# Feed-forward entry: own space for the first weights, banks and copy targets, three blocks begun ahead, and GpSimd on part of the last activations

## The chip, the core and the metric

The kernel runs on one core of a Trainium2 chip. A core has a matrix engine (TensorE, PE in the profile), a vector engine (VectorE, DVE), a scalar engine (ScalarE, ACT), GpSimd (POOL) and a queue engine (SyncE, SP) that here issues all transfers. On-chip memory is SBUF; matmuls write into the eight banks of PSUM. Every engine works through its own list of instructions in order and stops at a wait until a semaphore is reached. The metric is the device time of the run in microseconds; lower is better.

## The reference, cut to what matters

One transformer block on 1024 tokens of width 1024. A mixing half (dilated attention and a gated delta rule) gives `y`; the change lies behind it, where the residual is formed, normalised, and sent through the feed-forward layer:

```python
y = jnp.concatenate([y_attn, y_delta], axis=-1) @ w_out[l]
x = x + g1 * y
h = _rmsnorm(x, norm_ffn_g[l]) * (1.0 + sc2) + sh2
y = (jax.nn.silu(h @ w_gate[l]) * (h @ w_up[l])) @ w_down[l]
x = x + g2 * y
return _rmsnorm(x, final_norm_g)
```

`w_gate` and `w_up` are 1024 x 2816, `w_down` is 2816 x 1024, all in 32-bit floats.

## The kernel before, in words

**Precision.** Each matmul operand is split in two: a rounded high part (`...h`, made by a ScalarE cast) and the rest (`...l`, a subtraction of the high part from the source). A product is three matmuls: high x high, high x low, low x high. A slab of weights is 128 x 512; it takes a transfer, a cast (`wh`, line 1502) and a subtraction (`wl`, line 1503, on VectorE).

**Residual stage.** A first loop (line 1339) has already added half of the output projection. The loop at line 1415 runs over two halves of the tokens (`hf`, 512 tokens each) and eight tiles of the width (`d`). For each it splits a slab of `w_out` (`wsplit`: ring `wr` of three raw slabs, rings `wh` and `wl` of five, subtraction on GpSimd, line 216), runs 12 matmuls (line 567), adds the result to the residual tile `x2[d, hf]` on VectorE (line 1429), transposes the tile on TensorE for the later residual (`x2_turn`, lines 1382 to 1389, up to two tiles behind), and sums the squares: ScalarE squares, GpSimd or VectorE adds (lines 1437 to 1441).

**Norm.** After each half, eight tiny matmuls (`ssq`, line 1451) sum the squares over the partitions, ScalarE takes the root, VectorE the reciprocal, VectorE spreads it on a diagonal (`dg`, line 1454), TensorE broadcasts it (`rsb`, line 1458) and ScalarE copies it out (`rs`, line 1459). `normed2` (line 1469) scales each tile with `rs` on VectorE (line 1471) and adds the shift on ScalarE (line 1474). The first half's norm lies inside the second half's matmuls. The second half's lies at the end of the stage, ahead of all feed-forward matmuls.

**Feed-forward as seven products.** The layer's products are done by a scheme of seven products in place of eight, over a 2 x 2 division of weights (quarters `a11`, `a12`, `a21`, `a22`) and activations. The activation side needs seven operands of four tiles each, all split high and low: `H11` and `H21` (first token half alone, ready early) and `H22`, `T1`, `T2`, `T3`, `T4` (sums and differences that need the second token half). `h2_split` (line 1404) makes them: a ScalarE cast (line 1406) and a VectorE subtraction (line 1407). In the last of them, `T4`, VectorE does the cast as well. The differences are VectorE instructions of `sub` (line 1519).

**Order of the feed-forward work.** There are 11 blocks `f`, each with a gate side (`wg`) and an up side (`wu`). `up_first` (line 1526) does a side's two products with `H11` and `H21` (24 matmuls, banks `a` and `b`); `rest_begin` does `T2` and `T1` (24 matmuls, bank `c`), and `up_rest` does `T3`, `H22`, `T4` (36 matmuls), with copies `u2` and `r5` taken out of the banks between (lines 1566 and 1568). `AHEADF` blocks have their first parts done ahead (`early`, line 1639), since these need no second half; `begun` then starts block 0's rest; the loop over all blocks follows. A block begun ahead loads its raw slabs a second time for its rest. All these matmuls have the line 1513.

**What sets the order.** The program is written in order and a scheduler lays out each engine's list by priority (`urgent()` raises it); within a list the order is fixed when it runs. A tile that takes over memory of an earlier one waits until that one's last reader is done. Three such places matter here. The feed-forward weights' pool `wq` and the operands' pool `pt` lie where the residual stage's operands and weight slabs lay. The feed-forward banks `pq` lie where the banks of the stage before lay. And the pool `po2`, with `u2` and `r5`, is opened after `sx.close()`, so it lies where the residual tiles `x2` lay.

Of the kernel before, what the change touches and what calls it, by code (L numbers as in the profile page):

```python
# [18 lines left out]
P = 128  # L19
# [10 lines left out]
EARLY = 1  # L30
LEVELS = ("qd", 4), ("z1", 36)
TAIL = 4
AHEADF = 2
XB, ETB, AT, AV = 5, 4, 1, 3
EPS = 1e-6
BIG = 1e30
# [33 lines left out]
def build(tc, I, out):  # L70
# [21 lines left out]
    def urgent():  # L92
        return tc.high_priority(offset=6000)
# [1284 lines left out]
    pf, sf = pool("pf")  # L1378
    po, so = pool("po")
    ps_, ss_ = pool("ps_")  # L1380
    px, sx = pool("px")
    def x2_turn(d, hf, t):

        ps = tbank(f"x2t{d}_{hf}")
        for b in range(4):
            nc.tensor.transpose(ps[:, b * P : (b + 1) * P], t[:, b * P : (b + 1) * P], ident)
        xt = px.tile([P, 4, P], F32, name=f"xt2_{d}_{hf}", tag="m", bufs=5)
        nc.scalar.copy(xt.rearrange("p b d -> p (b d)"), ps)
# [10 lines left out]
    def h2_block(p, name):  # L1399
        HB[name] = [  # L1400
            tuple(p.tile([P, HALF], F32R, name=f"{name}{w}{k}", tag=f"{name}{w}{k}") for w in "hl") for k in range(4)
        ]

    def h2_split(name, k, src, lo_eng, copy=None):
        hi, lo = HB[name][k]
        (copy or nc.scalar.copy)(hi, src)
        lo_eng.tensor_tensor(out=lo, in0=src, in1=hi.bitcast(F32), op=ALU.subtract)
# [6 lines left out]
    for i, (ks, hf) in enumerate(((range(4), 0), (range(4), 1), (range(4, 8), 1), (range(4, 8), 0))):  # L1414
        for d in ks:
            x2[d, hf] = px.tile([P, HALF], F32, name=f"x2_{d}_{hf}", tag=f"x{i}", bufs=4)

    for hf in range(2):
        cs = slice(hf * HALF, (hf + 1) * HALF)
        if hf == 1:  # L1420
            acc = px.tile([P, HALF], F32, name="acc2_1", tag="m", bufs=5)
        for d in range(KT):
            slabs = [(wsplit(I["wo"][d, 0], 512, f"wo{d}_0_{hf}"), 0)]
            t = x2[d, hf]
            nc.sync.dma_start(t, _.xp[2 * d + hf])
            ps = (gbank, sbank)[d % 2](f"wo{d}_0_{hf}")
            run(gemm(ps, slabs, yh, yl, cs))
            with urgent():
                nc.vector.scalar_tensor_tensor(
                    out=t, in0=ps, scalar=mod[:, 16 + d : 17 + d], in1=t, op0=ALU.mult, op1=ALU.add,  # L1430
                )
            behind.append((d, hf, t))
            if len(behind) > 2:
                with tc.issue_after(last[0].ins):
                    x2_turn(*behind.pop(0))
            if d == 0:
                nc.scalar.activation(acc, t, AF.Square)
            else:
                sq = px.tile([P, HALF], F32, name=f"sq2_{hf}_{d}", tag="m", bufs=5)
                nc.scalar.activation(sq, t, AF.Square)  # L1440
                (nc.vector if d > 5 else nc.gpsimd).tensor_tensor(out=acc, in0=acc, in1=sq, op=ALU.add)
        while behind:
            x2_turn(*behind.pop(0))

        ps, pb = ybank(f"ssq2_{hf}"), abank(f"rsb2_{hf}")
        r4 = r8[:, 4 * hf : 4 * hf + 4]
        rs = po.tile([P, HALF], F32, name=f"rs2_{hf}", tag="p1", bufs=4)
        dg = po.tile([P, 4, P], F32, name=f"dg2_{hf}", tag="p1", bufs=4)
        with urgent():
            for tb in range(4):  # L1450
                nc.tensor.matmul(ps[:, tb : tb + 1], acc[:, tb * P : (tb + 1) * P], ones[:, 0:1], start=True, stop=True)
            nc.scalar.activation(r4, ps[:, 0:4], AF.Sqrt, bias=eps1, scale=1.0 / D)
            nc.vector.reciprocal(r4, r4)
            nc.vector.tensor_tensor(
                out=dg, in0=ident.unsqueeze(1).to_broadcast([P, 4, P]),
                in1=r4.unsqueeze(2).to_broadcast([P, 4, P]), op=ALU.mult,
            )
            nc.tensor.matmul(pb, ones, dg.rearrange("p b t -> p (b t)"), start=True, stop=True)
            nc.scalar.copy(rs, pb)
        if hf == 1:  # L1460
            sy.close()
            spv.close()
            swp.close()
            wq, swq = pool("wq", side="right")
            pt, st_ = pool("pt", side="right")
            for name in ("H22", "T1", "T2", "T3", "T4"):
                h2_block(pt, name)

        def normed2(d):
            t = x2[d, hf]  # L1470
            nc.vector.scalar_tensor_tensor(
                out=t, in0=t, scalar=G2[:, d : d + 1], in1=rs, op0=ALU.mult, op1=ALU.mult
            )
            nc.scalar.activation(t, t, AF.Identity, bias=mod[:, 24 + d : 25 + d])

        if hf == 0:
            for d in range(KT):
                normed2(d)
                h2_split(("H11", "H21")[d // 4], d % 4, x2[d, 0], nc.vector)


    spg.close()
    pq, spq = pool("pq", space=PSUM)

    def fbank(name):
        return pq.tile([P, HALF], F32, name=name, tag="f", bufs=8)

    def raw_load(src, name, more=False):
        if more:
# [16 lines left out]
    def up_mm(ps, src, name, what, first=True):  # L1506

        wh, wl = parts(src, name)
        for k in range(4):
            w0 = slice(k * P, (k + 1) * P)  # L1510
            bh, bl = HB[what][k]
            for n_, (a, b) in enumerate(((wh, bh), (wh, bl), (wl, bh))):
                nc.tensor.matmul(  # L1513
                    ps, a[:, w0], b, start=(first and k == 0 and n_ == 0), stop=(k == 3 and n_ == 2),
                    skip_group_check=True,
                )
# [6 lines left out]

    def up_first(f, w, raws):

        a, b = fbank(f"{w}a{f}"), fbank(f"{w}b{f}")
        up_mm(a, raws[0], f"{w}{f}_11", "H11")
        p1 = po.tile([P, HALF], F32, name=f"p1_{w}{f}", tag="p1", bufs=4)  # L1530
        with urgent():
            nc.scalar.copy(p1, a)
        up_mm(b, raws[1], f"{w}{f}_12", "H21")
        with urgent():
            add(p1, b, p1)
        return a, p1
# [18 lines left out]
    def up_rest(f, w, a, raws):  # L1555

        a11, a12 = raws
        if (f, w) == (0, "wg"):
            (s1, s2, a21, a22), c = rest0, begun
        else:  # L1560
            a21, a22 = (raw_load(I[w][NF + f, s], f"{w}{f}_2{s}", True) for s in range(2))
            s1, s2 = rest_sums(po2 if w == "wu" else ps_, f, w, raws, a21, a22)
            c = rest_begin(f, w, a, (s1, s2))
        u2, r5 = (po2.tile([P, HALF], F32, name=f"{w}{f}_u{i}", tag="u", bufs=4) for i in (2, 5))
        with urgent():
            nc.scalar.copy(u2, a)
# [15 lines left out]
    def gate_first(f, w):  # L1582
        raws = raws_first(f, w)
        a, c11 = up_first(f, w, raws)
        return a, c11, raws
# [58 lines left out]

    t2 = []
    for k in range(4):
        normed2(k)
        normed2(4 + k)
# [10 lines left out]
        sub(x2[k, 1], x2[4 + k, 1], x2[k, 1])  # L1659
        h2_split("T3", k, x2[k, 1], nc.vector)  # L1660
    for k in range(4):
        h2_split("H22", k, x2[4 + k, 1], nc.vector)
    for k in range(4):
        sub(x2[4 + k, 0], x2[4 + k, 0], t2[k])
        h2_split("T4", k, x2[4 + k, 0], nc.vector, nc.vector.tensor_copy)
    sx.close()
    po2, so2 = pool("po2")
    for f in range(NF):
        up_end(f, early[f] if f < AHEADF else None)
        for i in {0: (), 1: (), NF - 2: (NF - 4, NF - 3), NF - 1: (NF - 2, NF - 1)}.get(f, (f - 2,)):  # L1670
            wd_sums(i)
    so2.close()
    ss_.close()
    so.close()
    sf.close()
# [206 lines left out]
```

## Time and profile before

| what | value |
|---|---|
| median of three runs | 1454.71 us (1454.52 to 1459.43) |
| the profiled execution's own time | 1459.26 us |
| its span | 1457.5 us |
| TensorE busy | 1381.9 us (95%) |
| VectorE, ScalarE, GpSimd busy | 872.7, 668.8, 284.5 us |
| mean granted TensorE clock | 0.975 |
| feed-forward entry in the span | from about 798 to 856 us |

The span is counted from the first to the last instruction. A busy share is an average over stages of very different kinds. So the stretch around the entry is read by itself: TensorE's instructions in order of time show where it stops, the view of waits names what it stopped for, and the lists of VectorE, ScalarE and GpSimd in the same stretch show what they were doing. In the profile a timeline row is start, length, engine, line, operation, tiles written and read, and the idle time before it with what ended it. TensorE's rows overlap, since a matmul's result comes some time after the next has begun; the pace is the distance between starts. The rows of a table by stretch give the length, then for PE, PEld, DVE, ACT and POOL the busy time and (x) the instructions, then the granted TensorE clock, the DMA share and GB/s.

### The profile page before, as it was taken

To read this page: it belongs to the slowest core of one execution; us is meant where nothing else is said; L and a number is where in the kernel's file an instruction comes from. 1 tells how busy PE (TensorE), PEld (TensorE's weight loads), DVE (VectorE), ACT (ScalarE), POOL (GpSimd) and SP (SyncE) were. 2 spreads that over 40 slices of the span, in tenths; PEclk is the share of its full clock that TensorE was granted. 3 is DMA by queue.
4 is the path that set the end of the run, shared out by engine and by line. 5 is a ranking of instruction groups with operands and counts; after the bars stand their busy time and mean duration, and the time that the engine had idled before them with its cause. 6 is when DMAs were issued, how large, how long until landed. Compare 5 with 4: busy or idle time off the path is not lost.

```text
span 1457.5 us, 24558 instructions
## 1 busy us (share of the span) xinstructions
PE 1381.9 (95%) x8984; PEld 1121.6 (77%) x8984; DVE 872.7 (60%) x1676; ACT 668.8 (46%) x1279; POOL 284.5 (20%) x267
## 2 busy tenths in 40 slices
PE   7998989998999989999999889999999999999997
PEld 4777857787888768778877668888888888888886
DVE  3686762665746151466426985767666676565477
ACT  3487513348233363566337733333333333444446
POOL 1343412243323333344244000000000000000000
PEclk9998999998999989999999989999999999999999
DMA  8736464465531626643275443545454465866566
GB/s 306 251 106 175 134 192 142 146 197 168 157 107 56 179 78 181 169 121 95 92 226 168 136 151 117 192 137 175 148 167 156 155 207 182 277 211 202 198 218 238
DMA packets 171345, 244.64 MB, mean 168 GB/s; under 512 B 33014, under 2 KB 76327, under 8 KB 171224
## 3 DMA queue, kind: packets, MB, share of 16 engines
q1 hardware_dynamic: 171224, 243.07, 53.0%
q8 instruction: 71, 1.16, 0.3%
q14 instruction: 50, 0.41, 0.1%
HBM read 180.25 MB, written 67.48 MB: 170 GB/s over the span
## 4 chain that ended last, share of the span: by engine, by line
PE 63%; DVE 6%; DMA 4%; ACT 3%; issue 2%; POOL 1%; SPq 0%; ACTq 0%; DVEq 0%; POOLq 0%
PE wga L1513 8%; PE wua L1513 8%; PE X L1699 6%; PE g_a L567 5%; PE wuc L1513 4%; PE wgc L1513 4%; PE Z L1699 4%; PE wo L567 4%; PE g_va L590 3%; PE y L1293 3%; PE tr L1276 2%; PE Y L1699 2%; PE wub L1513 2%; PE wgb L1513 2%; PE S L1252 1%
## 5 line engine op out<-in xcount | busy, mean ns | idle before, releaser
L1503 DVE TENSOR_TENSOR wl_db<-wr_db,wh_db 128x512 fp32r<-128x512 f32 x77 | 53.2, 691 | 75.6 <-ACT wh_db L1502 75.5
L1502 ACT CAST wh_db<-wr_db 128x512 fp32r<-128x512 f32 x77 | 47.9, 622 | 97.8 <-PE X L1699 41.3
L1699 PE MATMUL X<-wl_db,wh_da 128*128 128x512 f32 x176 | 68.5, 389 | 0.0
L1699 PE MATMUL X<-wh_db,wl_da 128*128 128x512 f32 x176 | 68.5, 389 | 0.0
L1699 PE MATMUL X<-wh_db,wh_da 128*128 128x512 f32 x176 | 68.5, 389 | 0.0
L1263 POOL TENSOR_SCALAR X<-X,sc 128x128 f32<-128x128 f32 (+7 forms) x64 | 47.6, 747 | 70.6 <-DVE sc L1262 56.2
L1261 ACT ACTIVATE X<-X,sc 128x128 f32<-128x128 f32 (+7 forms) x64 | 49.6, 776 | 22.4 <-DVE sc L1256 17.2
L1256 DVE CUSTOM_DVE_ANT_0 X<-S,ng 128x512 f32<-128x512 f32 (+3 forms) x64 | 36.8, 586 | 35.0 <-PE S L1253 26.3
L567 PE MATMUL wo<-yh,wh_wo 128*128 128x512 f32 x128 | 52.2, 409 | 3.7 <-ACT yh L1359 2.1
L1503 DVE TENSOR_TENSOR wl_da<-wr_da,wh_da 128x512 fp32r<-128x512 f32 x77 | 52.7, 686 | 1.2 <-ACT wh_da L1502 1.2
L567 PE MATMUL g_a<-hh,wh_a 128*128 128x512 f32 x128 | 51.4, 401 | 0.0
L567 PE MATMUL g_a<-hl,wh_a 128*128 128x512 f32 x128 | 51.1, 399 | 0.0
L567 PE MATMUL g_a<-hh,wl_a 128*128 128x512 f32 x128 | 51.0, 398 | 0.0
L567 PE MATMUL wo<-yl,wh_wo 128*128 128x512 f32 x128 | 51.0, 398 | 0.0
L567 PE MATMUL wo<-yh,wl_wo 128*128 128x512 f32 x128 | 50.5, 396 | 0.0
L1502 ACT CAST wh_da<-wr_da 128x512 fp32r<-128x512 f32 x77 | 47.4, 616 | 5.9 <-PE wua L1513 5.8
L1222 DVE SCALAR_TENSOR_TENSOR QS<-raw,QS 64x1024 fp32r<-64x1024 f32 x8 | 12.6, 1571 | 61.4 <-ACT QS L1221 61.4
L1502 ACT CAST wh_wg_s<-wg_s 128x512 fp32r<-128x512 f32 x33 | 20.5, 622 | 58.1 <-PE wuc L1513 22.6
L1293 PE MATMUL y<-et,va 128*64 128x128 f32 x576 | 46.7, 289 | 0.0
L1276 PE MATMUL tr<-ident,X 128*128 128x128 f32 x288 | 45.0, 282 | 1.6 <-ACT et L1281 1.2
L1502 ACT CAST wh_wg<-wr_wg 128x512 fp32r<-128x512 f32 x33 | 20.4, 622 | 51.4 <-issue 20.0
L1293 PEld LDWEIGHTS y<-et,va 128*64 128x64 f32 x576 | 35.0, 142 | 10.4 <-issue 8.8
(530 smaller groups left out, 4391.4 us busy)
## 6 DMA issues: line engine op xcount, KB each, us to landing
wr_da<-ao_d SPq DMA_DIRECT2D x77, 256.0 KB, 3.1
wm<-in_wada SPq DMA_DIRECT2D x64, 256.0 KB, 3.6
wr_wg<-in_wg SPq DMA_DIRECT2D x48, 256.0 KB, 2.9
wr_wu<-in_wu SPq DMA_DIRECT2D x48, 256.0 KB, 2.7
ao_d<-a SPq DMA_DIRECT2D x44, 256.0 KB, 2.2
wr_wd<-in_wdn SPq DMA_DIRECT2D x44, 256.0 KB, 3.0
wr_db<-wt_d SPq DMA_DIRECT2D x44, 256.0 KB, 2.6
ao_d<-as SPq DMA_DIRECT2D x33, 256.0 KB, 2.0
```

Of the source, the lines that this page charges most:

```text
L567: last[0] = nc.tensor.matmul(ps, a[:, w0], b[k0 + k4][:, cs], start=(i == 0), stop=(i == n - 1))
L590: last[0] = nc.tensor.matmul(ps[:, :n], a[k][:, ts_], b[:, w0], start=(i == 0), stop=(i == 23))
L1252: nc.tensor.matmul(ps[:, 0 : c1 - c0], QS[:, qs], KS[:, c0:c1], start=True, stop=False)
L1256: nc.vector.tensor_tensor_reduce(out=X[:, c0:c1], in0=ps[:, 0 : c1 - c0], in1=ng[:, u + c0 : u + c1], scale=1.0, scalar=(3e38 if m is None ...
L1261: nc.scalar.activation(X[:, 0:nk], X[:, 0:nk], AF.Exp, scale=-1.0, bias=m, accum_out=sc[:, 2:3])
L1263: nc.gpsimd.tensor_scalar(out=X[:, 0:nk], in0=X[:, 0:nk], scalar1=sc[:, 3:4], scalar2=0.0, op0=ALU.mult, op1=ALU.add)
L1276: nc.tensor.transpose(ps[:, (kb - c0) * P : (kb - c0 + 1) * P], X[:, kb * P : kb * P + P], ident)
L1293: nc.tensor.matmul(yps[64 * e : 64 * e + 64, yc], va[:, kb, 64 * e : 64 * e + 64], ets[e][:, kb, :], start=(kb == 0), stop=(kb == qb),)
L1502: nc.scalar.copy(hi, src)
L1503: (eng or nc.vector).tensor_tensor(out=lo, in0=src, in1=hi.bitcast(F32), op=ALU.subtract)
L1513: nc.tensor.matmul(ps, a[:, w0], b, start=(first and k == 0 and n_ == 0), stop=(k == 3 and n_ == 2), skip_group_check=True,)
L1699: nc.tensor.matmul(bank[b], a[:, ts_], w, start=(first and f == 0 and n_ == 0), stop=(f == NF - 1 and n_ == 2), skip_group_check=True,)
```

## The change

- **First weights.** The two slabs of block 0's gate side are loaded, cast and subtracted during the second half of the residual stage (`slab_early`): the raw slabs pass through the residual stage's ring of three, the split ones have a pool of their own (`pe`), and the subtraction is on GpSimd.
- **Order at the entry.** The feed-forward banks are opened directly behind the residual stage. Block 0's gate side is begun first (24 matmuls), then the second half's norm (`norm2`, marked urgent) and the transposes left over come, each in a feed-forward bank.
- **Copy targets.** `rs` and `dg` of the norm and block 0's gate copies `u2` and `r5` have space in `pe`, not in memory that the residual tiles held. The ring `p1` has six places in place of four.
- **Ahead.** `AHEADF` is 3 in place of 2: the first parts of block 2 (48 matmuls) are done before block 0's rest.
- **GpSimd.** The four subtractions of `H22`, the four differences for `T4` and two of the four subtractions of `T4` go from VectorE to GpSimd; the four casts of `T4` go from VectorE to ScalarE.
- The scratch that the builder reserves in SBUF for dynamic DMA is set to 256 bytes a partition.

```diff
-AHEADF = 2
+AHEADF = 3
...
+    def norm2(hf, acc, ps, pb):
+        r4 = r8[:, 4 * hf : 4 * hf + 4]
+        rs = pe.tile([P, HALF], F32, name=f"rs2_{hf}", tag="u0", bufs=2)
+        dg = pe.tile([P, 4, P], F32, name=f"dg2_{hf}", tag="u0", bufs=2)
+        with urgent():
+            ...
+    def slab_early(s):
+        raw = wp.tile([P, slot], F32, name=f"er{s}", tag="wr", bufs=3)
+        hi = pe.tile([P, HALF], F32R, name=f"eh{s}", tag="eh", bufs=2)
+        lo = pe.tile([P, HALF], F32R, name=f"el{s}", tag="el", bufs=2)
+        nc.sync.dma_start(raw, I["wg"][0, s])
+        nc.scalar.copy(hi, raw)
+        nc.gpsimd.tensor_tensor(out=lo, in0=raw, in1=hi.bitcast(F32), op=ALU.subtract)
+        return hi, lo
...
         if hf == 1:
             acc = px.tile([P, HALF], F32, name="acc2_1", tag="m", bufs=5)
+            slabs0 = [slab_early(s) for s in range(2)]
...
+        if hf == 1:
+            break
         while behind:
             x2_turn(*behind.pop(0))
...
-        u2, r5 = (po2.tile([P, HALF], F32, name=f"{w}{f}_u{i}", tag="u", bufs=4) for i in (2, 5))
+        if (f, w) == (0, "wg"):
+            u2, r5 = (pe.tile([P, HALF], F32, name=f"{w}{f}_u{i}", tag="u0", bufs=2) for i in (2, 5))
+        else:
+            u2, r5 = (po2.tile([P, HALF], F32, name=f"{w}{f}_u{i}", tag="u", bufs=4) for i in (2, 5))
...
-    early = [{w: gate_first(f, w) for w in ("wg", "wu")} for f in range(AHEADF)]
+    a0, c0_ = up_first(0, "wg", (None, None), slabs0)
+    with urgent():
+        rs = norm2(1, acc, fbank("ssq2_1"), fbank("rsb2_1"))
+    while behind:
+        x2_turn(*behind.pop(0), bank=fbank)
+    early = [{w: gate_first(f, w) if (f, w) != (0, "wg") else (a0, c0_, None) for w in ("wg", "wu")} for f in range(AHEADF)]
...
     for k in range(4):
-        h2_split("H22", k, x2[4 + k, 1], nc.vector)
+        h2_split("H22", k, x2[4 + k, 1], nc.gpsimd)
     for k in range(4):
-        sub(x2[4 + k, 0], x2[4 + k, 0], t2[k])
-        h2_split("T4", k, x2[4 + k, 0], nc.vector, nc.vector.tensor_copy)
+        sub(x2[4 + k, 0], x2[4 + k, 0], t2[k], nc.gpsimd)
+        h2_split("T4", k, x2[4 + k, 0], nc.gpsimd if k < 2 else nc.vector)
...
-    nc = _bacc.Bacc("TRN2", target_bir_lowering=False, num_devices=1)
+    nc = _bacc.Bacc("TRN2", target_bir_lowering=False, num_devices=1, dynamic_dma_scratch_size=256)
```

More of the change, by code (lines that the diff above doesn't have):

```diff
@@ L1380, in build, with x2_turn @@
     ps_, ss_ = pool("ps_")
+    pe, se = pool("pe")
     px, sx = pool("px")
-    def x2_turn(d, hf, t):
-        ps = tbank(f"x2t{d}_{hf}")
+    def x2_turn(d, hf, t, bank=None):
+        ps = (bank or tbank)(f"x2t{d}_{hf}")
         for b in range(4):
@@ L1416, in build, with normed2 @@
             x2[d, hf] = px.tile([P, HALF], F32, name=f"x2_{d}_{hf}", tag=f"x{i}", bufs=4)
+    def norm2(hf, acc, ps, pb):
[3 more added lines that the diff above has]
+        with urgent():
+            for tb in range(4):
+                nc.tensor.matmul(ps[:, tb : tb + 1], acc[:, tb * P : (tb + 1) * P], ones[:, 0:1], start=True, stop=True)
+            nc.scalar.activation(r4, ps[:, 0:4], AF.Sqrt, bias=eps1, scale=1.0 / D)
+            nc.vector.reciprocal(r4, r4)
+            nc.vector.tensor_tensor(
+                out=dg, in0=ident.unsqueeze(1).to_broadcast([P, 4, P]),
+                in1=r4.unsqueeze(2).to_broadcast([P, 4, P]), op=ALU.mult,
+            )
+            nc.tensor.matmul(pb, ones, dg.rearrange("p b t -> p (b t)"), start=True, stop=True)
+            nc.scalar.copy(rs, pb)
+        return rs
+    def normed2(d, hf):
+        t = x2[d, hf]
+        nc.vector.scalar_tensor_tensor(
+            out=t, in0=t, scalar=G2[:, d : d + 1], in1=rs, op0=ALU.mult, op1=ALU.mult
+        )
+        nc.scalar.activation(t, t, AF.Identity, bias=mod[:, 24 + d : 25 + d])
+    def slab_early(s):
[6 more added lines that the diff above has]
+        return hi, lo
     for hf in range(2):
@@ L1441, in build @@
                 (nc.vector if d > 5 else nc.gpsimd).tensor_tensor(out=acc, in0=acc, in1=sq, op=ALU.add)
+        if hf == 1:
+            break
         while behind:
             x2_turn(*behind.pop(0))
[L1445 to L1479, printed above, removed]
+        rs = norm2(hf, acc, ybank(f"ssq2_{hf}"), abank(f"rsb2_{hf}"))
+        for d in range(KT):
+            normed2(d, hf)
+            h2_split(("H11", "H21")[d // 4], d % 4, x2[d, 0], nc.vector)
     spg.close()
@@ L1486, in fbank @@
         return pq.tile([P, HALF], F32, name=name, tag="f", bufs=8)
+    sy.close()
+    spv.close()
+    swp.close()
+    wq, swq = pool("wq", side="right")
+    pt, st_ = pool("pt", side="right")
+    for name in ("H22", "T1", "T2", "T3", "T4"):
+        h2_block(pt, name)
     def raw_load(src, name, more=False):
@@ L1504, in parts, with up_mm @@
         return hi, lo
-    def up_mm(ps, src, name, what, first=True):
-        wh, wl = parts(src, name)
+    def up_mm(ps, src, name, what, first=True, pr=None):
+        wh, wl = pr or parts(src, name)
         for k in range(4):
@@ L1522, in add, with up_first @@
         (eng or nc.vector).tensor_tensor(out=out, in0=a, in1=b, op=ALU.add)
-    def up_first(f, w, raws):
+    def up_first(f, w, raws, prs=(None, None)):
         a, b = fbank(f"{w}a{f}"), fbank(f"{w}b{f}")
-        up_mm(a, raws[0], f"{w}{f}_11", "H11")
-        p1 = po.tile([P, HALF], F32, name=f"p1_{w}{f}", tag="p1", bufs=4)
+        up_mm(a, raws[0], f"{w}{f}_11", "H11", pr=prs[0])
+        p1 = po.tile([P, HALF], F32, name=f"p1_{w}{f}", tag="p1", bufs=6)
         with urgent():
             nc.scalar.copy(p1, a)
-        up_mm(b, raws[1], f"{w}{f}_12", "H21")
+        up_mm(b, raws[1], f"{w}{f}_12", "H21", pr=prs[1])
         with urgent():
@@ L1646, in build @@
     for k in range(4):
-        normed2(k)
-        normed2(4 + k)
+        normed2(k, 1)
+        normed2(4 + k, 1)
         sub(x2[k, 0], x2[k, 1], x2[k, 0])
@@ L1672, in build @@
     so2.close()
+    se.close()
     ss_.close()
```

## The prediction

> **What bounds the kernel now.** I read the page's span and chain first, then the table by stretch, then TensorE's waits and timeline at the entry, and last the lists of VectorE and GpSimd there.
>
> ```profile
> span 1457.5 us, 24558 instructions
> ...
> PE 63%; DVE 6%; DMA 4%; ACT 3%; issue 2%; POOL 1%; SPq 0%; ACTq 0%; DVEq 0%; POOLq 0%
> ```
>
> The chain that ended last is mostly TensorE. The change touches one place, so the stretches around it come next.
>
> ```profile
> 742.00:798.36 56.36, 52.82 (x257) 42.29 (x256) 28.74 (x38) 34.33 (x60) 29.72 (x22) 1.00 0.62 199
> 798.36:834.30 35.94, 33.73 (x143) 26.53 (x141) 31.68 (x53) 26.40 (x48) 0.00 (x0) 0.91 0.50 154
> 834.30:845.30 11.00, 0.00 (x1) 0.01 (x1) 11.00 (x21) 2.40 (x5) 0.00 (x0) 0.73 0.44 140
> 845.30:862.00 16.70, 16.70 (x65) 13.63 (x66) 14.01 (x23) 7.22 (x13) 0.00 (x0) 0.87 0.36 119
> 862.00:1000.00 138.00, 138.00 (x610) 114.27 (x609) 92.05 (x145) 50.12 (x87) 0.00 (x0) 1.00 0.45 149
> ```
>
> The residual stage (first row) and the blocks (last row) keep TensorE busy. Between them it stands still for 11 us while VectorE is busy without a break, and around that the clock is below 1. GpSimd does nothing from 798 us on.
>
> ```profile
> PE wga L1513 <- ACT wg_u L1566: 11.0, 1, 11.0
> ```
>
> ```profile
> 843.29 1.22 DVE x L1519 x2
> ...
> 844.66 0.59 ACT wg_u L1566
> ...
> 845.30 5.03 PE wga L1513 x12
> ...
> 855.77 2.72 PE wua L1513 x12
> ```
>
> ```profile
> L1407 DVE TENSOR_TENSOR T3l<-x,T3h x4: 684/684/685, 834.7 to 838.3; 128x512 fp32r<-128x512 f32 x4
> ```
>
> That wait has two locks. The copy `u2` could not start before the last differences for `T4` were done, since it lies in memory of the residual tiles; and without that, VectorE would not have been done with `T3` before 839. The first 12 matmuls after the stop take 5.03 us where 12 take 2.72 us later (0.227 us each).
>
> ```profile
> 800.95 1.06 PE L1451 MATMUL ssq<-onesr,acc 128*128 128x1 f32 x8 [0.60 <-DVE acc L1441]
> 803.30 2.08 PE L1458 MATMUL rsb<-dg,onesr 128*128 128x512 f32 x2 [1.29 <-DVE dg L1454]
> 804.39 1.42 PE L1513 MATMUL wga<-H11h,wh_wg 128*128 128x512 f32 x1
> ...
> 812.31 0.39 PE L1513 MATMUL wua<-H11h,wh_wu 128*128 128x512 f32 x1
> ```
>
> This is the other loss: the norm's chain of small steps, with the first matmuls of the feed-forward behind it at a reduced clock.
>
> **Two limits for the new entry.** I count from 798.36 (last residual matmul) to the start of block 0's up-side rest, the row at 855.77 above. The changed kernel has by then done 48 matmuls more (block 2's first parts, 48 x 0.227 = 10.9 us), so the old kernel's equivalent point is 855.77 + 10.88 = 866.65.
>
> *TensorE alone.* 144 matmuls of first parts and 60 of block 0's gate rest: 204 x 0.227 = 46.3. Twelve transposes left over 1.6 (three groups of four, about half a microsecond each), `ssq` 1.06, `rsb` about 1.0 at full clock (half of 2.08). Sum 50.0, so 848.3. Nothing else at all would give 18.3 us of gain.
>
> *VectorE with GpSimd.* In the changed kernel's instruction order VectorE has 54 instructions from the first scaling by `rs` to the last `T3` subtraction, where the old one has 66 to its last `T4` subtraction. Fourteen leave (4 `H22`, 4 differences, 4 casts, 2 `T4`); block 2 adds six (4 slab subtractions, 2 sums of `p1`); four slab subtractions of blocks 0 and 1 now lie ahead of the stretch.
>
> ```profile
> 805.42 0.59 ACT L1459 COPY rs<-rsb 128x512 f32<-128x512 f32 x1 [1.56 <-PE rsb L1458]
> 806.04 0.75 DVE L1471 SCALAR_TENSOR_TENSOR x<-x,G,rs 128x512 f32<-128x512 f32 x1 [0.98 <-ACT rs L1459]
> 831.10 1.89 DVE L1407 TENSOR_TENSOR T1l<-x,T1h 128x512 fp32r<-128x512 f32 x3
> ```
>
> Back to back, three subtractions take 1.89 with the last one's tail, 0.60 each; an instruction of the scaling's kind takes 0.66 from start to start (782.34 to 783.00 below). Eight scalings and 46 others: 5.3 + 27.7 = 33.0. They begin where they begin now: `ssq` stands in TensorE's list behind 13 first matmuls and `rsb` behind 7 more, but at full clock; 798.4 + 0.5 + 2.9 + 1.1 + 1.6 + 1.0, plus 0.6 for `rs`, is 806.1 against 806.04.
>
> What GpSimd's ten instructions cost VectorE is the open price. The residual stage shows both at once:
>
> ```profile
> 778.75 1.96 DVE L1471 SCALAR_TENSOR_TENSOR x<-x,G,rs 128x512 f32<-128x512 f32 x2
> 780.63 1.78 DVE L1407 TENSOR_TENSOR H11l<-x,H11h 128x512 fp32r<-128x512 f32 x1
> 782.34 0.74 DVE L1429 SCALAR_TENSOR_TENSOR x<-wo,mod,x 128x512 f32<-128x512 f32 x1
> 783.00 1.12 DVE L1471 SCALAR_TENSOR_TENSOR x<-x,G,rs 128x512 f32<-128x512 f32 x1
> ```
>
> ```profile
> 780.19 1.67 POOL L1441 TENSOR_TENSOR acc<-acc,sq 128x512 f32<-128x512 f32 x1 [0.69 <-ACT sq L1440]
> 781.83 1.74 POOL L216 TENSOR_TENSOR wl_wo<-wr_wo,wh_wo 128x512 fp32r<-128x512 f32 x1
> ```
>
> ```profile
> L1441 POOL TENSOR_TENSOR acc<-acc,sq x10: 1284/1296/1672, 754.9 to 796.7; 128x512 f32<-128x512 f32 x10
> ```
>
> The `H11l` subtraction takes 1.78 beside GpSimd's sum, against 0.684 alone: 1.10 longer, nearly GpSimd's own 1.296. GpSimd's sum is longer too (1.67), by the rest of VectorE's instruction in front. The add from PSUM at 782.34 keeps its 0.74 beside GpSimd. So instructions with both inputs in SBUF take turns, and ten moved ones cost VectorE 10 x 1.10 = 11.0, where they saved 6.0 (ten at 0.60). Six of the 54 read PSUM; I let about one GpSimd instruction pass beside them: 9.7. Bounds: 0 and 13.0 (ten at 1.296). I take 9.7, since the row with 1.10 is the same pair of operations on the same sizes. The last `T3` part is then ready at 806.1 + 33.0 + 9.7 = 848.8. Behind it TensorE still has 2 matmuls of `T3`, 12 of `H22` and 12 of `T4`: 26 x 0.227 = 5.9, so 854.7. This is later than 848.3 and decides. Gain 866.65 - 854.7 = 12.0.
>
> On this the Trainium skill, "SBUF — State Buffer", section "Who interferes with whom", has a rule that speaks against moving work to GpSimd: a VectorE instruction with two SBUF inputs and a GpSimd instruction that reads SBUF exclude each other, and the later one is blocked for the whole of the other. By it the price is GpSimd's whole 1.296 with the same turns, the upper bound above, and the gain some 2 to 3 us smaller; the trace agrees on the turns and shows 1.10.
>
> **The clock.** TensorE will be without work for some 6 us (854.7 less 848.3) between about 837 and 849, in pieces of 1 to 3 us.
>
> ```profile
> 800.00:805.00 5.00, 3.11 (x15) 1.93 (x12) 3.31 (x6) 2.94 (x7) 0.00 (x0) 0.69 0.87 294
> ...
> 840.00:845.00 5.00, 0.00 (x0) 0.00 (x0) 5.00 (x11) 0.34 (x1) 0.00 (x0) 0.50 0.93 299
> ```
>
> ```profile
> 788.71 0.66 PE L1386 MATMUL x2t<-ident,x 128*128 128x128 f32 x4 [1.86 <-ACT xt L1388]
> ```
>
> Pieces of 0.60 and 1.29 with little work between took the clock down at 800 to 805 (0.69); a single stop of 1.86 at 787 did not (the first stretch has 1.00). One spell at half clock costs 5.03 - 2.72 = 2.3. Bounds 0 and 2.3; I take half, 1.1. The Trainium skill, "TensorE: Matmul & The Clock Gate", section "What's actually happening", says the clock falls after a whole idle window of about 3.4 us; by that these pieces would cost nothing, and the sum would be 1.1 better. The row at 800 differs from it: no stop there was that long.
>
> **The other edits.** *First weights:* two transfers, two casts and two GpSimd subtractions more in the residual stage, and the raw slabs share its ring of three.
>
> ```profile
> 770.52 0.33 SPq L214 DMA_DIRECT2D wr_wo<-in_wo  x1
> ```
>
> ```profile
> 795.50 0.49 PE L567 MATMUL wo<-yh,wh_wo 128*128 128x512 f32 x1
> ```
>
> ```profile
> wr_wg<-in_wg SPq DMA_DIRECT2D x48, 256.0 KB, 2.9
> ```
>
> The last residual slab is loaded 25 us ahead of its matmuls. The casts stand in ScalarE's list and make the following slab casts wait for these transfers: 2 x (2.9 + 0.6) = 7 us if uncovered; 25 us of lead cover it, so 0. *Order and banks:* the 24 matmuls now run inside the norm's waits; that is in the TensorE limit already. Three blocks hold six banks, block 0's `c` the seventh, the up side's `c` the eighth; the next `c` is wanted 13.6 us (60 x 0.227) after block 0's gate is done, so 0. *SP:* the last two transposed tiles are written out later, with the second loads of block 0 behind them; wanted ten microseconds on, 0. *Block 2's second load:* four transfers more, 4 x 2.9 = 11.6 us if uncovered, in a stretch with a DMA share of 0.45 and no wait of TensorE: 0. *ScalarE:* four casts of `T4` and block 2's six instructions, ten at some 0.6 or 6 us, where it was busy for 28.8 of the 46.9 us from 798.36 to 845.30: 0. *Copy targets:* `u2` no longer waits for the differences; the price is in the limits. Behind the entry TensorE has no wait, so what is won there reaches the end.
>
> **Sum.** 12.0 - 1.1 = 10.9 us. The profiled execution's own time is 1459.26, which gives 1448.4. It lies 4.55 above the median of the runs, 1454.71; from the median the forecast is 1443.8, say 1444.
>
> **The rivals.**
> 1. *GpSimd runs free of VectorE.* Then VectorE ends at 839 and TensorE's limit holds: 18.3, so 1436. The 0.74 beside GpSimd speaks for it, the 1.78 against. Chance 0.12.
> 2. *Turns at the full price, with a spell at half clock.* 13.0 for 9.7 makes 858.0; gain 8.7 - 2.3 = 6.4, so 1448. It is under 0.5% (7.3 us, about what the runs of this kernel, 4.9 us apart, can tell from no change). The same time would come of some 3 us of waits of VectorE on ScalarE's casts, which no row shows. Chance 0.23.
> 3. *GpSimd becomes the bound, and the kernel is slower.* At the place above, the ten GpSimd instructions would each have to hold VectorE for more than 2.0 us after the clock's 2.3.
>
> ```profile
> L216 POOL TENSOR_TENSOR wl_z<-wr_z,wh_z x8: 1268/1287/2272, 100.4 to 305.2; 128x512 fp32r<-128x512 f32 x8
> ```
>
> The longest row of such an instruction is 2.27: 22.7 for 9.7 makes 867.7, with the clock a loss of 3.4, so 1458. For slower by over 0.5% it takes about 2.7 each. Its median of 1.287 speaks against it. Chance 0.08, of which 0.05 beyond 2.7.
>
> **How the numbers follow.** My forecast has the rest, 0.57. Faster by over 0.5% are the forecast and rival 1: 0.69; within 0.5% are rival 2 and the nearer part of rival 3: 0.26; slower 0.05. The range goes from rival 1 (1436, and half a microsecond of it left out) to 1452, past rival 2's 1448 by the spread of 4 us in the runs. The forecast's own range is 1440 to 1447.
>
> **What would show it.** Right: `wga` starts at about 799 ahead of `ssq`; TensorE's 11 us wait is gone, with several of 1 to 3 us in its place at about 837 to 849, put down to VectorE's `T2l` and `T3l`; GpSimd shows ten instructions between 813 and 838; VectorE's rows there are up to 1.8 us; block 0's up-side rest starts at about 855 with block 2 begun. Wrong: VectorE rows at 0.68 beside GpSimd (rival 1), GpSimd rows over 2 us with VectorE still (rival 3), or a stop of TensorE inside the residual stage.

## The result, and the profile after

The changed kernel took 1446.69 us in the median (1439.76 to 1457.62, 13 runs) beside 1458.55 us for the kernel before (1452.59 to 1463.75, 13 runs). The ratio is 0.9936 with a 95% interval of 0.9913 to 0.9958: faster, by about 9 us. The forecast was 1444 from a median of 1454.71, which is a ratio of 0.9926. The kernel was run again later beside the experiments and gave 0.9920 (0.9893 to 0.9947).

The profiled execution took 1446.69 us. Its page has the span and the shares of the chain that ended last:

```profile
span 1445.0 us, 24561 instructions
...
PE 62%; DVE 6%; DMA 5%; ACT 3%; issue 2%; POOL 1%; SPq 0%; DVEq 0%; ACTq 0%; POOLq 0%
```

The page as a whole hardly differs. The table by stretch does (columns as before: length, PE, PEld, DVE, ACT, POOL busy with instruction counts, granted clock, DMA share, GB/s). The first row begins behind the last residual matmul, as 798.36 did before:

```profile
795.85:834.30 38.45, 38.28 (x177) 31.26 (x175) 36.53 (x46) 28.57 (x51) 15.41 (x10) 1.00 0.46 144
834.30:845.30 11.00, 7.52 (x23) 5.14 (x23) 11.00 (x18) 5.05 (x10) 0.81 (x1) 0.84 0.13 41
845.30:862.00 16.70, 15.68 (x67) 12.44 (x68) 14.70 (x25) 7.80 (x15) 0.00 (x0) 1.00 0.62 205
862.00:1000.00 138.00, 138.00 (x610) 114.28 (x609) 98.23 (x155) 49.02 (x84) 0.00 (x0) 1.00 0.52 168
```

TensorE works through the norm at full clock, and in the 11 us in which it stood still it is now busy for 7.5. VectorE is still busy without a break there. TensorE's waits between 796 and 862 us (total, times, longest) say what is left:

```profile
PE wga L1525 <- DVE T2l L1408: 2.2, 1, 2.2
PE wga L1525 <- ACT wg_u L1581: 0.8, 1, 0.8
PE wga L1525 <- DVE T3l L1408: 0.7, 1, 0.7
PE wgc L1525 <- DVE p_wg L1534: 0.5, 1, 0.5
PE wua L1525 <- DVE wl_wu_s L1515: 0.3, 1, 0.3
```

In place of one wait of 11 us there are six of at most 2.2 (the last, 0.3 for a cast, isn't shown). TensorE's timeline gives the entry its marks: last residual matmul, block 0's gate side ahead of the norm, the last part of `T3`, and block 0's up-side rest.

```profile
795.62 0.39 PE L567 MATMUL wo<-yh,wl_wo 128*128 128x512 f32 x1
795.85 0.60 PE L1387 MATMUL x2t<-ident,x 128*128 128x128 f32 x4
796.20 0.48 PE L1525 MATMUL wga<-H11h,eh 128*128 128x512 f32 x1
...
799.29 0.95 PE L1425 MATMUL ssq<-onesr,acc 128*128 128x1 f32 x8
...
846.53 0.50 PE L1525 MATMUL wga<-T3l,wh_wg_s 128*128 128x512 f32 x1 [0.66 <-DVE T3l L1408]
...
852.56 0.39 PE L1525 MATMUL wua<-T2h,wh_wu_s 128*128 128x512 f32 x1
```

From here on "entry" is the time from the start of the last residual matmul to the start of the first `T2` matmul on the up side. It is 852.56 - 795.62 = 56.9 us. Before, it was 855.61 - 798.13 = 57.5, and 68.4 with the 10.9 us of block 2's 48 matmuls. So 11.4 us were won there:

```profile
798.13 0.39 PE L567 MATMUL wo<-yh,wl_wo 128*128 128x512 f32 x1
...
855.61 0.39 PE L1513 MATMUL wua<-T2h,wh_wu_s 128*128 128x512 f32 x1
```

VectorE's rows in the stretch show what holds TensorE now, and GpSimd's rows show why:

```profile
803.49 0.75 DVE L1438 SCALAR_TENSOR_TENSOR x<-x,G,rs 128x512 f32<-128x512 f32 x1
...
816.08 1.78 DVE L1438 SCALAR_TENSOR_TENSOR x<-x,G,rs 128x512 f32<-128x512 f32 x1
...
823.61 1.78 DVE L1408 TENSOR_TENSOR T2l<-t,T2h 128x512 fp32r<-128x512 f32 x1
...
845.80 0.68 DVE L1408 TENSOR_TENSOR T3l<-x,T3h 128x512 fp32r<-128x512 f32 x1
```

```profile
815.63 3.39 POOL L1531 TENSOR_TENSOR x<-x,t 128x512 f32<-128x512 f32 x2 [3.64 <-DVE t L1531]
821.78 4.75 POOL L1408 TENSOR_TENSOR H22l<-x,H22h 128x512 fp32r<-128x512 f32 x3 [2.75 <-ACT H22h L1407]
```

Instructions with both inputs in SBUF that take 0.68 or 0.74 alone take up to 1.78 while GpSimd works. Ten of VectorE's rows are lengthened in this way: eight by 1.04 to 1.10 us, and two, which start right behind an add from PSUM, by 0.72 and 0.51. Together that is 9.9 us. From the first scaling to the end of the last `T3` subtraction VectorE needs 846.48 - 803.49 = 43.0 us.

### The profile page after: what moved, and what is told of

It reads as the page before. It is cut to its first block, busy times and chain, and to the rows that moved or that the text cites. A ratio compares the mean times of both kernels' runs of the same rounds, so it can differ in the third digit from the quotient of the medians.

```text
span 1445.0 us, 24561 instructions
## 1 busy us (share of the span) xinstructions
PE 1379.9 (95%) x8984; PEld 1119.5 (77%) x8984; DVE 873.4 (60%) x1660; ACT 670.0 (46%) x1283; POOL 305.2 (21%) x279
## 4 chain that ended last, share of the span: by engine, by line
PE 62%; DVE 6%; DMA 5%; ACT 3%; issue 2%; POOL 1%; SPq 0%; DVEq 0%; ACTq 0%; POOLq 0%
PE wua L1525 8%; PE wga L1525 8%; PE X L1720 6%; PE g_a L567 5%; PE wuc L1525 4%; PE Z L1720 4%; PE wgc L1525 4%; PE g_va L590 4%; PE wo L567 2%; PE y L1293 2%; PE tr L1276 2%; PE Y L1720 2%; PE wgb L1525 2%; PE wub L1525 2%; PE S L1252 1%
## 5 line engine op out<-in xcount | busy, mean ns | idle before, releaser
L1515 DVE TENSOR_TENSOR wl_da<-wr_da,wh_da 128x512 fp32r<-128x512 f32 x77 | 52.7, 685 | 1.2 <-ACT wh_da L1514 1.2
L567 PE MATMUL g_a<-hl,wh_a 128*128 128x512 f32 x128 | 51.1, 399 | 0.0
L1252 PE MATMUL S<-KS,QS 128*128 128x512 f32 (+3 forms) x96 | 36.9, 394 | 7.3 <-ACT KS L1226 4.9
L216 POOL TENSOR_TENSOR wl_wo<-wr_wo,wh_wo 128x512 fp32r<-128x512 f32 x24 | 32.0, 1337 | 50.8 <-ACT wh_wo L215 40.7
```

Of the source, the lines that this page charges most:

```text
L567: last[0] = nc.tensor.matmul(ps, a[:, w0], b[k0 + k4][:, cs], start=(i == 0), stop=(i == n - 1))
L1252: nc.tensor.matmul(ps[:, 0 : c1 - c0], QS[:, qs], KS[:, c0:c1], start=True, stop=False)
```

## The experiments

All times below are ratios to the kernel before, from the same group of runs, with 95% intervals. Profiled executions reached the entry at anything from 791.9 to 803.6 us, and the same kernel once at 794.2 and once at 803.6; so profiles are compared by the entry's length, not by the clock time in the span.

**GpSimd's ten instructions.** First all of them on VectorE, the rest as changed:

```diff
-        h2_split("H22", k, x2[4 + k, 1], nc.gpsimd)
+        h2_split("H22", k, x2[4 + k, 1], nc.vector)
...
-        sub(x2[4 + k, 0], x2[4 + k, 0], t2[k], nc.gpsimd)
-        h2_split("T4", k, x2[4 + k, 0], nc.gpsimd if k < 2 else nc.vector)
+        sub(x2[4 + k, 0], x2[4 + k, 0], t2[k])
+        h2_split("T4", k, x2[4 + k, 0], nc.vector)
```

> The changed kernel with the ten instructions of GpSimd at the entry back on VectorE (the four casts of T4 stay on ScalarE). Theory of turns: a moved instruction cost VectorE about 1.10 us of waiting where it saved 0.60, so VectorE gets done earlier without GpSimd. From the first scaling to the last T3 subtraction it takes at most 33 + 6 = 39 us instead of the 43.0 of the changed kernel (803.49 to 846.48); TensorE's waits there, 4.9 us in all, shrink to under 2; the run is 3 to 5 us faster than the changed kernel, about 0.990 of the kernel before. Rival, the offload earns: VectorE has ten instructions more, 6 us, so T3 comes 3 to 6 us later, the waits grow and the ratio is about 0.997.

Measured: 0.9911 (0.9878 to 0.9944). The entry took 51.1 us. That run reached the entry 8 us later than the changed kernel's profile, so it was repeated beside the changed kernel in one group:

> The changed kernel itself, run beside the next three so that they have one yardstick. From the start of the last residual matmul to the start of block 0's first T2 matmul on the up side it took 56.9 us (before: 57.5, or 68.4 with block 2's 48 matmuls added). Expected of all theories: the same again, 56 to 58 us, 0.9936 of the time before within 0.002.

> All ten GpSimd instructions on VectorE, as in the experiment before. In its first profile the entry took 51.1 us against 56.9, and VectorE's stretch from the first scaling to the last T3 subtraction 33.1 us against 43.0. Theory (the ten instructions cost VectorE 9.9 us ahead of T3, and the work they take over was not due before T3): entry 51, so about 6 us better than the changed kernel, 0.9895 of the time before. Rival (the 8 us by which that run reached the entry later than the changed kernel's belong to it, and what is won at the entry is lost in the residual stage): no better than the changed kernel, 0.9936, with the entry again reached at about 804 us.

Measured: the changed kernel 1445.72 us, 0.9920 (0.9893 to 0.9947), entry 57.0; all on VectorE 1441.65 us, 0.9894 (0.9867 to 0.9921), entry 51.1 again, reached at 794.2. The late arrival did not belong to the kernel. The intervals overlap, so the time alone leaves it likely only; the entry is shorter by 5.9 us in both profiles, and the median by 4.1. Its timelines and all its waits of TensorE from 794 to 862 us:

```profile
794.15 0.39 PE L567 MATMUL wo<-yh,wl_wo 128*128 128x512 f32 x1
...
845.24 0.50 PE L1525 MATMUL wua<-T2h,wh_wu_s 128*128 128x512 f32 x1 [1.25 <-ACT wh_wu_s L1514]
```

```profile
802.02 0.75 DVE L1438 SCALAR_TENSOR_TENSOR x<-x,G,rs 128x512 f32<-128x512 f32 x1 [0.21 <-ACT rs L1433]
...
834.48 0.69 DVE L1408 TENSOR_TENSOR T3l<-x,T3h 128x512 fp32r<-128x512 f32 x1
```

```profile
PE wua L1525 <- ACT wh_wu_s L1514: 1.2, 1, 1.2
PE wua L1525 <- DVE wl_wu_s L1515: 0.4, 1, 0.4
```

VectorE's stretch is 33.1 us instead of 43.0, so ten GpSimd instructions cost it 9.9. The stretch has 54 instructions in both kernels: two subtractions of `T4` stand in it in the changed kernel, two of `H22` here. The rest of `H22` and all of `T4` VectorE does behind the last of `T3` now, where nothing waits for it yet. TensorE does not wait inside the gate side at all: this is TensorE's own limit. From the point where the prediction counts (0.23 us behind the start of the last residual matmul) it is 50.9 us, 1.25 of them the last wait, where the prediction had 50.0.

Then the two halves of the edit, each alone on GpSimd:

> Only the four H22 subtractions are on GpSimd; differences and subtractions of T4 are on VectorE. Theory of turns: VectorE's stretch to the last T3 subtraction is 33.1 + 4 x 0.99 = 37.1 us. TensorE is not held by VectorE until about 2.8 + 1.25 us are used up (in the run with all on VectorE T3 was ready 10.1 us before the up rest began, where 26 matmuls and the wait of 1.25 make 7.2), so the entry stays at 50.5 to 51.5 us and the time at 0.9895. Rival (any GpSimd work at this place is paid in full on the path): entry 55, 0.992.

> Only T4's four differences and two of its subtractions are on GpSimd; the H22 subtractions are on VectorE. Theory of turns: stretch 33.1 + 6 x 0.99 = 39.0 us, entry 7.9 + 39.0 + 6.1 = 53 us, 0.991 of the time before. Rival (the price is that of H22 alone, since three of those come in a row in the middle of VectorE's chain): entry 51, 0.9895. Rival (paid in full on the path): entry 57, 0.9936.

Measured: `H22` alone 0.9890 (0.9862 to 0.9917), entry 52.5; `T4` alone 0.9900 (0.9867 to 0.9933), entry 52.7. First scaling and last `T3` subtraction of the two:

```profile
805.40 0.75 DVE L1438 SCALAR_TENSOR_TENSOR x<-x,G,rs 128x512 f32<-128x512 f32 x1 [0.21 <-ACT rs L1433]
...
841.66 0.68 DVE L1408 TENSOR_TENSOR T3l<-x,T3h 128x512 fp32r<-128x512 f32 x1
```

```profile
799.80 0.75 DVE L1438 SCALAR_TENSOR_TENSOR x<-x,G,rs 128x512 f32<-128x512 f32 x1
...
837.41 0.68 DVE L1408 TENSOR_TENSOR T3l<-x,T3h 128x512 fp32r<-128x512 f32 x1
```

From start to start that is 36.3 and 37.6, against 32.5 with none and 42.3 with ten: 3.8 us for four, 5.2 for six, 9.9 for ten. For four and for ten the price is about 1 us per instruction, all of it longer VectorE rows. For the six it is put together otherwise: four rows are longer, by 3.4 us in all, and 1.8 us are a wait of VectorE for a ScalarE cast. That cast stands in ScalarE's list behind one that waits for a GpSimd difference:

```profile
821.97 4.69 POOL L1531 TENSOR_TENSOR x<-x,t 128x512 f32<-128x512 f32 x1 [6.64 <-DVE t L1531]
```

```profile
826.69 0.62 ACT L1407 CAST T4h<-x 128x512 fp32r<-128x512 f32 x1 [2.34 <-POOL x L1531]
```

```profile
827.87 0.69 DVE L1515 TENSOR_TENSOR wl_wg_s<-wr_wg,wh_wg_s 128x512 fp32r<-128x512 f32 x1 [1.76 <-ACT wh_wg_s L1514]
```

The difference takes 4.69 us, where such rows take 1.3 to 1.8 in the changed kernel, and five VectorE instructions with both inputs in SBUF that start beside it keep their 0.60 from start to start. So here GpSimd was held and VectorE was not: the two exclude each other, but not always in strict turns. The expected 53 us came out in part by luck. In all of these, most of the price is hidden while TensorE is not waiting for VectorE; `H22` alone came out 1 us longer at the entry than expected, with waits of 0.9 for a bank's sum and 0.7 for `T3`. By time these two and the kernel with all on VectorE can't be told apart.

The edit alone (with `T4`'s casts on ScalarE, which belong to it), in the kernel before:

> The kernel before with the GpSimd part of the change alone. Theory of turns: VectorE's list loses 10 x 0.60 + 4 x 0.34 = 7.4 us and gets 10 x 1.10 = 11 us of waiting, so the entry (last residual matmul to block 0's up-side rest, 57.4 us before) gets 1 to 5 us longer: ratio 1.001 to 1.004. VectorE's instructions beside GpSimd show 1.7 to 1.8 us. Rival, the offload earns: the entry gets 4 to 7 us shorter, ratio 0.995 to 0.997.

Measured: 1.0029 (1.0007 to 1.0051), slower, as the theory of turns expected. The entry is 858.52 - 799.92 = 58.6 us. VectorE's 52 instructions to the last `T3` subtraction take 41.7 us, where the same 52 took 33.0. TensorE's waits there show the mechanism: the 11 us at `wg_u` shrink to 2.5, and 8 us of waits for `T2` take their place.

```profile
PE wga L1513 <- DVE T2l L1407: 4.0, 2, 2.4
PE wga L1513 <- ACT T2h L1406: 4.0, 1, 4.0
PE wga L1513 <- ACT wg_u L1566: 2.5, 1, 2.5
```

**The third block ahead.** `AHEADF = 2` in the changed kernel.

> The changed kernel with two blocks begun ahead. If the third block fills time in which TensorE would wait for VectorE: TensorE comes 10.9 us earlier to T2, T1 and T3, VectorE's list is six instructions (3.6 us) shorter, so its waits grow by about 7 us, to 12 or more, and the run is 7 us slower than the changed kernel: ratio about 0.9985. Rival, the block ahead is worth nothing, since VectorE sets the end and its list gets longer by it: ratio as the changed kernel, 0.9936. Second rival, it is worth all of its 10.9 us: ratio 1.001.

Measured: 0.9993 (0.9977 to 1.0010). The entry is 53.77 us, or 64.65 with the 10.88 of the 48 matmuls that it lacks, against 56.94: 7.7 longer. Without them TensorE is early and waits for the same VectorE, 10.3 us in all where 12 or more were expected (4.7 in the changed kernel). The three longest waits:

```profile
PE wga L1525 <- ACT T2h L1407: 3.9, 1, 3.9
...
PE wgc L1525 <- DVE T1l L1408: 2.6, 1, 2.6
...
PE wga L1525 <- DVE T2l L1408: 1.8, 1, 1.8
```

So block 2's matmuls are what the prediction takes them for, work for a TensorE that would stand: of their 10.9 us, 7.7 come back at the entry.

**First weights and order.** Both undone (no early slabs, norm and transposes ahead of the gate side):

```diff
-            slabs0 = [slab_early(s) for s in range(2)]
...
-    a0, c0_ = up_first(0, "wg", (None, None), slabs0)
...
-    early = [{w: gate_first(f, w) if (f, w) != (0, "wg") else (a0, c0_, None) for w in ("wg", "wu")} for f in range(AHEADF)]
+    early = [{w: gate_first(f, w) for w in ("wg", "wu")} for f in range(AHEADF)]
```

> The changed kernel with the old order at the entry: norm and transposes ahead of all feed-forward matmuls, and block 0's first slabs loaded with the others; three blocks ahead, the copy targets and GpSimd stay. Theory that VectorE with GpSimd sets the end: TensorE has about 5 us to spare, rs comes at the same time or 0.5 us later, and VectorE has the two slab subtractions again (1.2 us): 1 to 3 us slower than the changed kernel, ratio 0.994 to 0.996. Rival, the order at the entry is the main gain: its 4.8 us of waits and the spell at half clock (2.3) come back in full, 7 us, ratio about 0.9985.

Measured: 0.9996 (0.9974 to 1.0018): the expectation missed, and the rival was nearer. The entry is 861.05 - 794.63 = 66.4 us, 9.5 longer. VectorE's `T3` accounts for 1.8 of it (52.7 us from the last residual matmul to the end of the last `T3` subtraction, against 50.9): four slab subtractions more. The chain of waits and the timelines show the rest:

```profile
846.12 0.61 DVE wl_wg L1514
846.74 0.02 issue
846.75 0.33 SPq L1505
...
847.61 4.79 DMA wr_wu<-in_wu
```

```profile
852.49 0.69 DVE L1533 TENSOR_TENSOR wu_s<-wr_wu,wr_wu 128x512 f32<-128x512 f32 x1 [3.96 <-DMA wr_wu<-in_wu]
...
855.03 0.68 DVE L1533 TENSOR_TENSOR wg_u<-wga,wg_u 128x512 f32<-128x512 f32 x1
```

```profile
855.77 0.79 PE L1524 MATMUL wga<-T4h,wh_wg 128*128 128x512 f32 x1 [4.01 <-DVE wg_u L1533]
```

The second loads of block 0's up side stand one behind the other in SyncE's list. One of them waits for a ring place that VectorE's last slab subtraction of the blocks ahead frees; the one that is needed first is issued behind it and takes 4.8 us. In VectorE's list the first sum with that slab stands ahead of the sum that frees bank `a` for `T4`, so TensorE waits 4.0 us for a slab that it does not need yet; and the 12 matmuls behind take 861.05 - 855.77 = 5.28 where 2.72 is the pace. 1.8 + 4.0 + 2.6 = 8.4; the other 1.1 goes with a wait of 2.2 for `u2`'s copy. In the changed kernel the same chain is there and just fits: VectorE waits 0.44 us for the slab, and TensorE does not wait for the bank:

```profile
842.80 0.67 DVE L1515 TENSOR_TENSOR wl_wg<-wr_wg,wh_wg 128x512 fp32r<-128x512 f32 x1
...
847.52 0.69 DVE L1534 TENSOR_TENSOR wu_s<-wr_wu,wr_wu 128x512 f32<-128x512 f32 x1 [0.44 <-DMA wr_wu<-in_wu]
848.13 0.69 DVE L1534 TENSOR_TENSOR wg_u<-wga,wg_u 128x512 f32<-128x512 f32 x1
```

If so, a VectorE that is free 10 us sooner should take the chain away. The same old order with all ten instructions on VectorE:

> All ten GpSimd instructions on VectorE, and the first weights and the order as before (no early slabs, norm and transposes ahead of block 0's gate side). With GpSimd this order cost 9.5 us at the entry (66.4 against 56.9): 1.8 by VectorE, and the rest because the up side's slab came late into a ring place that VectorE freed last, with half clock behind it. Theory (without GpSimd VectorE frees that place some 10 us sooner, so only TensorE's unfilled norm is left; 24 matmuls were done 4.6 us earlier in the changed kernel): entry 51.1 + 4.6 = 55.7, ratio 0.9925. Rival (the order costs its 9.5 us whatever VectorE does): entry 60.6, 0.996.

Measured: 0.9917 (0.9886 to 0.9948), entry 857.33 - 801.02 = 56.3 us. TensorE's waits are those of the norm (2.0 and 1.3) and 1.2 for the up side's slab; no wait for `T4`. So the old order costs 5.2 us there and 9.5 in the changed kernel.

Early slabs kept, and only the order undone:

```diff
-    a0, c0_ = up_first(0, "wg", (None, None), slabs0)
     with urgent():
         rs = norm2(1, acc, fbank("ssq2_1"), fbank("rsb2_1"))
     while behind:
         x2_turn(*behind.pop(0), bank=fbank)
+    a0, c0_ = up_first(0, "wg", (None, None), slabs0)
```

> The changed kernel with its early slabs, but with the norm and the transposes ahead of block 0's gate side. Theory (both parts of the order edit matter: the norm's gap stays unfilled, but two slab subtractions fewer lie in VectorE's stretch, and two loads fewer pass the ring): entry 60 to 64 us, between 56.9 and the 66.4 without the early slabs; ratio 0.995 to 0.9975. Rivals: the weights' own space alone does it (57, 0.993); the order alone does it (66, 0.9996).

Measured: 0.9965 (0.9943 to 0.9987), entry 865.40 - 803.22 = 62.2 us, within the theory's 60 to 64. Both parts of the edit count, by one profile each: some 4 us the early slabs, some 5 the order.

**Copy targets.** `u2` and `r5` of block 0's gate side back in `po2`:

```diff
-        if (f, w) == (0, "wg"):
-            u2, r5 = (pe.tile([P, HALF], F32, name=f"{w}{f}_u{i}", tag="u0", bufs=2) for i in (2, 5))
-        else:
-            u2, r5 = (po2.tile([P, HALF], F32, name=f"{w}{f}_u{i}", tag="u", bufs=4) for i in (2, 5))
+        u2, r5 = (po2.tile([P, HALF], F32, name=f"{w}{f}_u{i}", tag="u", bufs=4) for i in (2, 5))
```

> Block 0's gate copies u2 and r5 lie again in the memory of the residual tiles (pool po2); the rest is the changed kernel. Then u2 has to wait for T4's last subtraction on VectorE, which ended at 845.9 where u2 was copied at 842.2. Theory (u2 is late by 3.7 us; TensorE stops there and does all 36 matmuls of T3, H22 and T4 behind it, 36 x 0.227 = 8.2, where 26 were left before): 2.1 us, up to 4.4 with one spell at half clock; entry 59 to 61 us, ratio some 0.0015 to 0.003 above the changed kernel's 0.993, so 0.9945 to 0.996. Rival (the place of the copies was only one of two locks, and VectorE is the one that holds now): entry 57, 0.993.

Measured: 0.9968 (0.9948 to 0.9987), entry 860.59 - 800.23 = 60.4 us. The entry is as expected, the ratio a little above. The stop, in TensorE's timeline:

```profile
850.85 0.80 PE L1525 MATMUL wga<-T3h,wh_wg_s 128*128 128x512 f32 x1 [5.35 <-ACT wg_u L1578]
```

The wait is not the one that was named. The copy starts at 850.22, directly behind ScalarE's last cast of `T3`; `T4`'s last subtraction ends only at 850.86.

The same with all on VectorE:

> All ten GpSimd instructions on VectorE, and the gate copies u2 and r5 in the memory of the residual tiles. Without GpSimd, VectorE does T4 behind T3: its last subtraction ended 6.8 us after the last of T3, so u2 waits until then. Theory: T3 on TensorE starts 7 us later than without this edit, with up to 2.3 for half clock; entry 58 to 60 us against 51.1, ratio 0.994 to 0.996 against 0.9894. GpSimd's work is then worth something only while the copies wait for T4. Rival (the copies' place does not matter): entry 51, 0.9894.

Measured: 0.9936 (0.9913 to 0.9959), entry 857.85 - 800.04 = 57.8 us. Both are just below what was expected. The stop in TensorE's timeline:

```profile
847.88 0.80 PE L1525 MATMUL wga<-T3h,wh_wg_s 128*128 128x512 f32 x1 [6.16 <-ACT wg_u L1578]
```

It lasts 6.2 us; the copy follows directly behind ScalarE's last cast of `T4`, not behind VectorE's last subtraction, which is why it is less than 7. The copies' own place is worth 6.7 us at the entry without GpSimd's work and 3.4 with it. By the entry (60.4 against 57.8) GpSimd did not pay even with the copies in their old place; by time the two intervals overlap.

Not run by themselves were the casts of `T4` on ScalarE, the space of `rs` and `dg`, the larger ring `p1` and the scratch setting; what each is worth is not shown.

## Why the prediction was right, point by point

- **Start of VectorE's stretch** (7.7 us behind the last residual matmul, unchanged): 803.49 - 795.85 = 7.6. Right.
- **54 instructions, 33.0 us:** 33.1 with GpSimd silent. Right.
- **GpSimd's price, 9.7** (turns at 1.10 each, about one hidden): 9.9. Right, and by the mechanism named: eight rows longer by 1.04 to 1.10 and two by 0.72 and 0.51, those behind an add from PSUM, where the prediction let one instruction in ten pass. Strict turns are too simple, as the run with six shows. The Trainium skill, "SBUF — State Buffer", section "Who interferes with whom", has the other engine blocked for the whole of the instruction. By it ten would have cost 13.0, an estimate from ten rows of 1.296; the trace agrees that the two hold each other up (VectorE 1.78, GpSimd 1.70), and the measured 9.9 decides. (At the full price the gain falls by 858.0 - 854.7 = 3.3, where the prediction's sentence on the Trainium skill has 2 to 3.)
- **VectorE's limit decides, not TensorE's:** yes, by 5.9 us. The last part of `T3` starts at 846.53 and the up side 6.0 later (5.9 forecast). From the prediction's starting point the up rest begins 56.7 us on, where VectorE's limit gave 56.3; of the gain of 12.0 at the entry 11.6 came. TensorE stands 4.7 us in six pieces, of which only one is over 1 us; the prediction had some 6 us in pieces of 1 to 3.
- **The clock, 1.1:** this term was wrong in place. The clock did fall (0.84 in the second row of the table by stretch), after a stop of 2.18 and one of 0.47, but among the matmuls ahead of the last `T3` part. TensorE had to wait for VectorE behind them anyway, so it cost nothing of the 56.7.
- **What won at the entry reaches the end:** nearly. In the two profiles, with block 2's 10.9 us included, the up rest began 13.9 us sooner and the span is 12.5 shorter. Of the 13.9, 2.5 lie ahead of the entry, where two profiles of one kernel were 9.4 apart. TensorE has no wait to speak of behind it, and where the 1.4 goes stays open. Over the thirteen comparisons with the kernel before, the ratio times 1457 gives on average 1.7 us less gain than the entry does. So the 1.1 taken off for the clock did not come, and a loss behind the entry that was not forecast stood in its place: that the sum of 10.9 is so near is in this part luck.
- **The other edits, costed at 0:** in the changed kernel they are. The residual stage shows no new stop of more than 0.8, and the banks and ScalarE cause none of more than 0.8. For the loads the cover was named too generously ("wanted ten microseconds on"): the up side's slab comes just in time, and without the early slabs and the order it makes TensorE stop for 4 us.
- **The rivals.** GpSimd free of VectorE fell with the rows of 1.78. The full price fell with 9.9 for 13.0. Its other road, VectorE waiting for ScalarE's casts, is not in the changed kernel's stretch, but the run with six shows it (1.8). A GpSimd that holds VectorE for 2.0 us per instruction did not come.
- **What the prediction did not see:** the edit with GpSimd is a loss inside a gain. The sum treated it as a price to be paid; but the work moved was not due before `T3`, so nothing was bought with it. TensorE's limit, which the prediction gave to the rival with a free GpSimd, is reached with an idle one.

## What to carry to other kernels

Moving ten instructions from a busy engine to an idle one did not pay here, since eight of them did not stand ahead of anything awaited. Before such a move look at what the receiver's work does to the shared engine's list before the awaited instruction, and not at its sum of busy time. Parts of a change that remove locks on the same spot do not add up: here the third block, the first weights with the order, and the copies, each taken back alone, gave up 7.7, 9.5 and 3.4 of the 11.4 us won at the entry, 20.6 in sum. A slab that arrives with little margin is a lock, too, if its first use stands in an engine's list ahead of something urgent.

## What the hardware showed that was not expected

The clock did not follow the stops alone. In the kernel before with only GpSimd's edit, the norm has the same stops at the same distances as before (0.29, 0.60 and 1.29 us); there `rsb` took 1.13 us and the clock stayed at 1.00, where before it was 2.08 and 0.75. The rows by stretch of the two kernels, before first:

```profile
798.36:805.40 7.04, 4.85 (x24) 3.25 (x23) 4.39 (x8) 3.88 (x8) 0.00 (x0) 0.75 0.74 240
```

```profile
800.15:807.20 7.05, 4.86 (x28) 3.61 (x27) 4.45 (x8) 4.94 (x10) 0.00 (x0) 1.00 0.76 243
```

After single stops of 5.35 and 4.01 us the next 12 matmuls took 4.28 and 5.28 us from start to start instead of 2.72; after one of 2.18 in the changed kernel the first two ran at full pace and the fall came a microsecond later, behind a further 0.47. The slow spell in the changed kernel lasts from 837.5 to about 840.6, some 3 us, and that behind the stop of 4.01 from 855.8 to about 862, some 6. The Trainium skill, "TensorE: Matmul & The Clock Gate", section "What's actually happening", has activity judged in windows of about 3.4 us that run freely of the kernel. The different outcomes of equal stops would fit that; no run here shows a window itself. For a sum, short stops near each other are better entered as a loss of 0 or of some 2 us, each with a chance, than as a mean that no run shows.
